# One value chain for layer one instead of two lanes of generators: two head groups in flight, outputs copied out of PSUM and gated in place

## The chip, the cores and the metric

The kernel runs on one core of a Trainium2 chip. The metric is the device time of one execution in microseconds (us), as a median over runs: 1005.12 us for the kernel before, from three runs of 1004.0, 1005.12 and 1005.37 us.

## The reference, cut to what matters

Two layers, 256 tokens, model width 2048, 16 heads of 128. The change lies in the first layer, a gated DeltaNet, between its input projection and its output projection:

```python
q, k, v = split(silu(causal_depthwise_conv(proj[..., :3 * 2048])))   # 4 taps
z = proj[..., 3 * 2048:4 * 2048]
...
o = linear attention with decay over chunks, from q, k, v            # per head
o = rms_norm(o, out_norm_w) * silu(z)
h = x + o.reshape(t, 2048) @ w_out                                   # then layer two
```

The kernel has already solved the triangular systems when the part of interest begins, and treats the 256 tokens as two blocks of 128. Per head it needs the values `v` after convolution and SiLU, a product with the inverse (twice, with a correction between them), a product with the decayed query-key matrix, a norm over 128 elements, the gate with `z`, and a transposition back to features by tokens.

## The kernel before

**The stream of weights.** 168 MB of weights pass through once, in 320 *chunks* of 512 KB, counted here from 0. `chunk` (helper `mm`, L255 in the profile) multiplies one chunk into a PSUM accumulator `psp`; there are two of those. `fetch` brings chunk i+3 when chunk i is about to be multiplied: a DMA on SP's queue into `wt` (4 buffers), a cast on ACT to a rounded copy `whi` (L206, 3 buffers), and the remainder on DVE as `wlo` (L207, 3 buffers). The cast of chunk i+3 takes the buffer that chunk i had, so it waits for the end of the matmuls that read that buffer.

**The background.** Everything else is written as generators in two lanes, `bgq` and `bg2`. After so many matmuls `tick` calls `step`, which advances one lane's first generator to its next `yield`. `yield 1` uses the step up; `yield 0` says "nothing done" and gives the step to the other lane. A scheduler then orders each engine's instructions. It may move them against the written order, matmuls of one accumulator against those of the other as well. Each engine runs its own list strictly in order.

**Chunks around the change.** Chunks 64 to 87 are z for head groups 0 to 2, 88 to 119 are v (eight chunks a group), 120 to 127 are z for group 3 (`za_small(3)`). Chunks 128 to 143 are the first half of the output projection: six chunks for accumulator 0 (128 to 133), six for accumulator 1 (134 to 139), then the last two of each (140, 141 and 142, 143). Here each chunk has 24 matmuls of 128x256 (two `whi`, one `wlo`, eight times). It reads 2 of the 16 heads of the gated output `g`, so accumulator 0 and 1 both go through head groups 0, 1, 2 (two chunks each), and chunks 140 to 143 need group 3. `ready(gmem)` writes background steps until the heads exist. `drain()` empties both lanes ahead of chunk 140.

**The value chain of one head group** (four heads, `gi` = 0 to 3):
- `v_conv` (lane `bg2`): convolution (L516, L518), one SiLU over all four heads (L806);
- `v_rest` (lane `bgq`): transposes (PE L823) and scaling (DVE L825) into `vb`; block 0 of the solve (PE L835, ACT copy L837 into `vs`); correction (PE L842, DVE L845); block 1 of the solve (L835, L837). It then puts `v_back` in lane `bg2`;
- `v_back` (lane `bg2`): output products into two PSUM tiles `po` (PE L858 to L860), squares straight from PSUM (ACT L861), their sums (DVE L868, L869), the power -0.5 on POOL (L871), scale and gate, reading `po` (DVE L885; for group 3 DVE L877), then `gated`: transposes (PE L897), and the halves of `g` (ACT L901, DVE L902).

The four work tiles `vb`, `vs`, `on`, `sq` are the same ones for each group (`dl_work(0)` to `dl_work(3)`). Two flags, `turned` and `back`, hold a group until the one ahead is far enough. For group 3 `za_small(3)`, in lane `bgq`, multiplies by z (DVE L780) and calls `gated`. All small PSUM tiles, `po` too, come from one pool `pss` of four banks.

In the profile an fp32 matmul of `order`'s lists (L835, L842, L858 to L860) shows as two instructions, a transpose as one.

Of the kernel before, what the change touches and what calls it, by code (L numbers as in the profile page):

```python
# [38 lines left out]
def tile_hybrid_trunk(  # L39
# [469 lines left out]
    def conv(src, i0):  # L509

        raw = wk("raw", 1)
        scaled(raw, src, scales["x"][1])
        cv = wk("cv")
        yield cv
        for i in range(4):
            act.activation(out=cv[:, i, :], in_=raw[:, i, :], func=AF.Copy, scale=conv_w(i0 + i, 3))  # L516
            for s in (1, 2, 3):
                dve.scalar_tensor_tensor(out=cv[:, i, s:], in0=raw[:, i, :T - s], scalar=conv_w(i0 + i, 3 - s),  # L518
                                         in1=cv[:, i, s:], op0=ALU.mult, op1=ALU.add)
# [248 lines left out]
    def za_small(gi, ps):  # L768
        if gi == 0:
            zmem["z"] = slot("kT", 16).rearrange("p (t d) -> p t d", t=2)  # L770
        for t in range(2):
            act.activation(out=zmem["z"][:, t, 512 * gi:512 * (gi + 1)], in_=ps[:, t, :], func=AF.Silu,
                           scale=scales["x"][0][:, t:t + 1])
        yield 1
        if gi == 3:
            while not gmem["on"]:
                yield 1
            on = dl_work(2)
            for t in range(2):
                dve.tensor_tensor(out=on[:, :, t, :], in0=on[:, :, t, :],  # L780
                                  in1=zmem["z"][:, t, 1536:].rearrange("p (h d) -> p h d", d=P), op=ALU.mult)
            yield 1
            yield from gated(3)
# [4 lines left out]
    def gated_tiles():  # L788
        gmem["b"] = slot("g", 32, F32R).rearrange("p (h a t) -> p h a t", h=H, a=2)
        gmem["h"], gmem["l"] = (gmem["b"][:, :, a, :] for a in range(2))  # L790
# [5 lines left out]
                step()  # L796
        return pre

    vmem = {"turned": -1, "back": -1}

    def v_conv(gi, ps):
        while vmem["turned"] < gi - 2:
            yield 1
        for cv in conv(ps, 32 + 4 * gi):
            yield 1
        act.activation(out=cv, in_=cv, func=AF.Silu)  # L806
        vmem[gi] = cv
        yield 1

    def v_rest(gi):  # L810
        while gi not in vmem:
            yield 1
        cv = vmem[gi]
        if gi == 0:
            gated_tiles()
        vb, vs, on, sq = (dl_work(k) for k in range(4))
        tt, l01, z = tmem["tt"], dl[:, :, 0, P:2 * P], zmem["z"]
        h0 = 4 * gi
        for p in range(2):
            ps = ps_small()  # L820
            for i in range(2):
                for t in range(2):
                    pe.transpose(ps[:, i * T + t * P:i * T + (t + 1) * P],  # L823
                                 cv[:, 2 * p + i, t * P:(t + 1) * P], ident)
            dve.tensor_tensor(out=vb[:, 2 * p:2 * p + 2], in0=ps.rearrange("p (h t d) -> p h t d", h=2, t=2),  # L825
                              in1=rk[:, h0 + 2 * p:h0 + 2 * p + 2, :].unsqueeze(3).broadcast_to([P, 2, 2, P]),
                              op=ALU.mult)
        vmem["turned"] = gi
        yield 1
        while vmem["back"] < gi - 1:  # L830
            yield 1
        for t in range(2):
            ps = ps_small()
            for i in range(4):
                pe.matmul(ps[:, i * P:(i + 1) * P], lhsT=tt[:, 2 * (h0 + i) + t, :], rhs=vb[:, i, t, :],  # L835
                          start=True, stop=True)
            act.copy(out=vs[:, :, t, :], in_=ps.rearrange("p (h d) -> p h d", d=P))  # L837
            yield 1
            if t == 0:
                ps = ps_small()  # L840
                for i in range(4):
                    pe.matmul(ps[:, i * P:(i + 1) * P], lhsT=l01[:, h0 + i, :], rhs=vs[:, i, 0, :],  # L842
                              start=True, stop=True)
# [4 lines left out]
                yield 1
        bg2.append(v_back(gi))

    def v_back(gi):
        vb, vs, on, sq = (dl_work(k) for k in range(4))
        z, h0 = zmem["z"], 4 * gi
        po = [ps_small(), ps_small()]
        for p in range(2):
            for i in (2 * p, 2 * p + 1):
                a, o = dec[:, h0 + i, :], po[p][:, (i % 2) * T:(i % 2 + 1) * T]
                pe.matmul(o[:, 0:P], lhsT=a[:, 0:P], rhs=vs[:, i, 0, :], start=True, stop=True)  # L858
                pe.matmul(o[:, P:T], lhsT=a[:, P:T], rhs=vs[:, i, 0, :], start=True, stop=False)
                pe.matmul(o[:, P:T], lhsT=a[:, T:T + P], rhs=vs[:, i, 1, :], start=False, stop=True)  # L860
            act.activation(out=sq[:, 2 * p:2 * p + 2], in_=po[p].rearrange("p (h t d) -> p h t d", h=2, t=2),  # L861
                           func=AF.Square)
# [6 lines left out]
        dve.scalar_tensor_tensor(out=so, in0=so, scalar=1.0 / P, in1=epq[:, h0:h0 + 4, :],  # L869
                                 op0=ALU.mult, op1=ALU.add)  # L870
        pool.tensor_tensor(out=ro, in0=so, in1=nhalf[:, :8].rearrange("p (h t) -> p h t", t=2), op=ALU.pow)  # L871
        yield 1
        yield 1
        if gi == 3:

            for p in range(2):
                dve.tensor_tensor(out=on[:, 2 * p:2 * p + 2], in0=po[p].rearrange("p (h t d) -> p h t d", h=2, t=2),  # L877
                                  in1=ro[:, 2 * p:2 * p + 2, :].unsqueeze(3).broadcast_to([P, 2, 2, P]), op=ALU.mult)
            gmem["on"] = True
            yield 1  # L880
            return
        for i in range(4):
            for t in range(2):
                c = (i % 2) * T + t * P
                dve.scalar_tensor_tensor(out=on[:, i, t, :], in0=po[i // 2][:, c:c + P], scalar=ro[:, i, t:t + 1],  # L885
                                         in1=z[:, t, (h0 + i) * P:(h0 + i + 1) * P], op0=ALU.mult, op1=ALU.mult)
        yield 1
        yield 1
        yield from gated(gi)

    def gated(gi):
        on, h0 = dl_work(2), 4 * gi
        for p in range(2):
            ps = ps_small()
            for i in range(2):
                for t in range(2):
                    pe.transpose(ps[:, i * T + t * P:i * T + (t + 1) * P], on[:, 2 * p + i, t, :], ident)  # L897
# [3 lines left out]
            act.activation(out=gh, in_=ps, func=AF.Copy, scale=sm[:, C_ONW:C_ONW + 1])  # L901
            dve.scalar_tensor_tensor(out=gl, in0=ps, scalar=sm[:, C_ONW:C_ONW + 1], in1=gh.bitcast(F32),  # L902
                                     op0=ALU.mult, op1=ALU.subtract)
        gmem["done"] = h0 + 4
        yield 1
# [350 lines left out]
```

## Time and profile before

| | |
|---|---|
| median of 3 runs | 1005.12 us |
| the profiled execution | 1003.71 us, its span 1002.0 us |
| PE matmul busy | 991.1 us, 99% |
| DVE busy | 686.0 us, 68% |
| ACT busy | 533.2 us, 53% |
| POOL busy | 71.6 us, 7% |
| mean of HBM read and written | 178 GB/s |

Busy time is what the profiler attributes to an engine. A matmul's end is modelled and overlaps the next matmul, so 99% for PE does not mean that nothing is lost; start-to-start times show more. PE's own chain makes up 95% of the chain that ended last.

### The profile page before, as it was taken

The page shows a single profiled execution, that of the slowest core. Times are in us where ns is not written, and L with a number is a line of the kernel's source. Part 1 is how long each engine was busy: PE and PEld are TensorE (multiplying, and loading weights), DVE is VectorE, ACT ScalarE, POOL GpSimd, SP SyncE. Part 2 cuts the span into 40 slices and gives each one's busy share as a digit, 9 for nine tenths or more (in the row PEclk, how much of TensorE's full clock was granted, in tenths as well). Part 3 has the DMA queues.
Part 4 walks back from the last instruction along what each step waited for, and adds up shares of the span by engine and source line. Part 5 has one row for each costly group of instructions (what it writes and reads, how often), then busy time and mean ns, then how long its engine had stood idle before and what let it go on. Part 6 is the DMA issues. An engine that isn't in the chain of part 4 may idle for free.

```text
span 1002.0 us, 15323 instructions
## 1 busy us (share of the span) xinstructions
PE 991.1 (99%) x5915; PEld 861.8 (86%) x5915; DVE 686.0 (68%) x1114; ACT 533.2 (53%) x757; POOL 71.6 (7%) x97
## 2 busy tenths in 40 slices
PE   9999999999999999999999999999999999999998
PEld 7988888888888898988888888888888888888887
DVE  7789788997999778655767555556565656555554
ACT  8456886646456555434664444446464645444442
POOL 1003000131000000001000000110101010000000
PEclk9999999999999999999999999999999999999999
DMA  9668775555765445435666766665556565555672
GB/s 290 188 174 250 208 205 153 148 169 151 205 191 169 130 145 157 141 106 169 229 188 179 233 201 212 199 177 167 175 161 187 151 188 148 168 170 172 215 218 87
DMA packets 138953, 179.67 MB, mean 179 GB/s; under 512 B 8048, under 2 KB 98560, under 8 KB 138880
## 3 DMA queue, kind: packets, MB, share of 16 engines
q1 hardware_dynamic: 136832, 172.12, 57.6%
q0 software_dynamic: 1760, 6.31, 1.8%
q8 instruction: 46, 0.75, 0.3%
q10 hardware_dynamic: 288, 0.26, 0.1%
q14 instruction: 27, 0.22, 0.1%
HBM read 176.56 MB, written 2.11 MB: 178 GB/s over the span
## 4 chain that ended last, share of the span: by engine, by line
PE 95%; ACT 1%; DVE 1%; DMA 1%; issue 1%; SPq 0%
PE psp L255 85%; PE pss L601 2%; DMA wt<-in_a_w_in_dram 1%; PE pss L255 1%; PE pss L1059 1%; PE pss L1079 1%; PE pss L1135 1%; ACT whi L206 1%; PE pss L835 1%; DVE wlo L207 1%; PE pss L1105 1%; PE pss L737 0%; PE pss L823 0%; PE pss L860 0%; PE pss L842 0%
## 5 line engine op out<-in xcount | busy, mean ns | idle before, releaser
L207 DVE TENSOR_TENSOR wlo<-wt,whi 128x1024 fp32r<-128x1024 f32 (+2 forms) x324 | 390.7, 1210 | 257.4 <-ACT whi L206 255.9
L206 ACT CAST whi<-wt 128x1024 fp32r<-128x1024 f32 (+2 forms) x324 | 336.7, 1040 | 380.5 <-PE psp L255 336.1
L255 PE MATMUL psp<-whi,xb 128*128 128x512 f32 x1024 | 319.1, 392 | 0.0
L255 PE MATMUL psp<-xb,whi 128*128 128x512 f32 (+1 forms) x1088 | 257.2, 379 | 0.5 <-ACT whi L206 0.2
L255 PEld LDWEIGHTS psp<-whi,xb 128*128 128x128 f32 x1024 | 192.1, 188 | 39.0
L255 PEld LDWEIGHTS psp<-xb,whi 128*128 128x128 f32 x1088 | 195.0, 189 | 34.7 <-ACT whi L206 0.9
L255 PE MATMUL psp<-wlo,xb 128*128 128x512 f32 x512 | 200.7, 392 | 0.0
L255 PE MATMUL psp<-xb,wlo 128*128 128x256 f32 x1024 | 147.1, 284 | 0.8 <-DVE wlo L207 0.7
L255 PEld LDWEIGHTS psp<-xb,wlo 128*128 128x128 f32 x1024 | 136.5, 191 | 7.0 <-DVE wlo L207 1.7
L255 PE MATMUL psp<-g,whi 128*128 128x512 f32 (+1 forms) x608 | 134.0, 348 | 2.2 <-ACT whi L206 1.3
L255 PEld LDWEIGHTS psp<-g,whi 128*128 128x128 f32 x608 | 104.7, 190 | 15.6 <-ACT whi L206 1.5
L255 PEld LDWEIGHTS psp<-wlo,xb 128*128 128x128 f32 x512 | 96.2, 188 | 19.4
L255 PE MATMUL psp<-g,wlo 128*128 128x256 f32 x480 | 82.5, 284 | 1.2 <-DVE wlo L207 1.2
L255 PEld LDWEIGHTS psp<-g,wlo 128*128 128x128 f32 x480 | 69.7, 191 | 3.6 <-DVE wlo L207 1.8
L518 DVE SCALAR_TENSOR_TENSOR cv<-raw,sm,cv 128x255 f32<-128x255 f32 (+2 forms) x144 | 64.3, 480 | 3.1 <-ACT cv L516 2.6
L516 ACT ACTIVATE cv<-raw,sm 128x256 f32<-128x256 f32 x48 | 22.4, 502 | 13.0 <-DVE raw L341 13.0
L326 DVE TENSOR_TENSOR ev<-psp,ev 128x512 f32<-128x512 f32 x37 | 25.2, 682 | 0.1
L325 ACT COPY ev<-psp 128x512 f32<-128x512 f32 x37 | 21.4, 579 | 2.6 <-DVE raw L341 2.5
L1042 POOL TENSOR_SCALAR ssn<-ssn,uh 128x4 f32<-128x4 f32 x16 | 9.3, 593 | 171.4 <-DVE ssn L1040 171.4
L871 POOL TENSOR_TENSOR ro<-so,nhalf 128x8 f32<-128x8 f32 x4 | 7.5, 1871 | 144.5 <-DVE so L869 144.5
L605 DVE TENSOR_TENSOR dl<-pss,dl 128x512 f32<-128x512 f32 (+1 forms) x32 | 16.4, 546 | 1.6 <-PE pss L601 1.6
L1049 DVE TENSOR_TENSOR cv<-psp,rn 128x512 f32<-128x512 f32 x16 | 10.3, 684 | 9.2 <-POOL rn L1044 9.2
(236 smaller groups left out, 730.3 us busy)
## 6 DMA issues: line engine op xcount, KB each, us to landing
wt<-in_b_w_in_dram SPq DMA_DIRECT2D x128, 512.0 KB, 3.8
wt<-in_a_w_in_dram SPq DMA_DIRECT2D x125, 512.0 KB, 4.0
wt<-in_a_w_out_dram SPq DMA_DIRECT2D x32, 512.0 KB, 3.6
wt<-in_b_w_out_dram SPq DMA_DIRECT2D x32, 512.0 KB, 3.5
tt<-line POOLq DMA_DIRECT2D x4, 512.0 KB, 8.4
dl<-in_xT_dram POOLq DMA_DIRECT2D x4, 512.0 KB, 6.3
dl<-in_relb_dram POOLq DMA_DIRECT2D x4, 512.0 KB, 4.9
g<-in_xT_dram SPq DMA_DIRECT2D x7, 256.0 KB, 6.4
```

The lines of the kernel that those rows point to most:

```text
L206: cast = act.copy(out=hi[:, js, cs], in_=wt[:, js, cs])
L207: rest = dve.tensor_tensor(out=lo[:, js, cs], in0=wt[:, js, cs], in1=hi[:, js, cs].bitcast(F32), op=ALU.subtract)
L255: state["mm"] = pe.matmul(*args, **kw).ins
L325: act.copy(out=ev, in_=ps[:, :, 1, :])
L326: dve.tensor_tensor(out=ev, in0=ps[:, :, 0, :], in1=ev, op=ALU.add)
L516: act.activation(out=cv[:, i, :], in_=raw[:, i, :], func=AF.Copy, scale=conv_w(i0 + i, 3))
L518: dve.scalar_tensor_tensor(out=cv[:, i, s:], in0=raw[:, i, :T - s], scalar=conv_w(i0 + i, 3 - s), in1=cv[:, i, s:], op0=ALU.mult, op1=ALU.add)
L601: pe.matmul(dst, lhsT=kq[:, a, i, c:c + P], rhs=rhs, start=(n == 0), stop=(n == 2))
L605: dve.tensor_tensor(out=dl[:, h, :, c], in0=src.rearrange("p (k c) -> p k c", k=2), in1=dec[:, h, c].unsqueeze(1).broadcast_to([P, 2, n]), ...
L835: pe.matmul(ps[:, i * P:(i + 1) * P], lhsT=tt[:, 2 * (h0 + i) + t, :], rhs=vb[:, i, t, :], start=True, stop=True)
L1049: dve.tensor_tensor(out=n[:, t, :].rearrange("p (h d) -> p h d", d=P), in0=ps[:, t, :].rearrange("p (h d) -> p h d", d=P), in1=rn[:, t, :] ...
L1059: pe.transpose(pt[:, i * T + t * P:i * T + (t + 1) * P], n[:, t, c:c + P], ident)
```

## The change

`v_rest` and `v_back` become one generator `v_chain` in lane `bgq`, written for all groups: transposes of group gi, outputs of group gi-1, solve of group gi, gate of group gi-1. Two groups are in flight, so `vb` alternates between two work tiles, and `vs` of groups 1 to 3 lies in `tt`, over the inverse blocks that the group before has used up. The flag `back` goes; waiting generators give their step away (`yield 0`). The SiLU is issued in two halves, as soon as two heads are convolved. The outputs are copied from PSUM into `on` (ACT L862), squared from there (L863), and scaled and gated in place in `on`. `za_small(3)` moves to lane `bg2`.

```diff
     def za_small(gi, ps):
...
             while not gmem["on"]:
-                yield 1
+                yield 0
...
     def v_conv(gi, ps):
         while vmem["turned"] < gi - 2:
-            yield 1
-        for cv in conv(ps, 32 + 4 * gi):
-            yield 1
-        act.activation(out=cv, in_=cv, func=AF.Silu)
+            yield 0
+        for n, cv in enumerate(conv(ps, 32 + 4 * gi)):
+            if n in (2, 4):
+                act.activation(out=cv[:, n - 2:n], in_=cv[:, n - 2:n], func=AF.Silu)
+            yield 1
         vmem[gi] = cv
...
+    def v_bufs(gi):
+
+        vb = dl_work(3 * (gi % 2))
+        vs = dl_work(1) if gi == 0 else tmem["tt"][:, 8 * gi - 8:8 * gi, :].rearrange("p (h t) d -> p h t d", t=2)
+        return vb, vs, dl_work(2)
...
-        while vmem["back"] < gi - 1:
-            yield 1
...
-        bg2.append(v_back(gi))
-
-    def v_back(gi):
-        vb, vs, on, sq = (dl_work(k) for k in range(4))
-        z, h0 = zmem["z"], 4 * gi
-        po = [ps_small(), ps_small()]
+
+    def v_out(gi):
+        (sq, vs, on), h0 = v_bufs(gi), 4 * gi
         for p in range(2):
+            po, pair2 = ps_small(), slice(2 * p, 2 * p + 2)
             for i in (2 * p, 2 * p + 1):
-                a, o = dec[:, h0 + i, :], po[p][:, (i % 2) * T:(i % 2 + 1) * T]
+                a, o = dec[:, h0 + i, :], po[:, (i % 2) * T:(i % 2 + 1) * T]
...
-            act.activation(out=sq[:, 2 * p:2 * p + 2], in_=po[p].rearrange("p (h t d) -> p h t d", h=2, t=2),
-                           func=AF.Square)
-        vmem["back"] = gi
-        yield 1
-
+            act.copy(out=on[:, pair2], in_=po.rearrange("p (h t d) -> p h t d", h=2, t=2))
+            act.activation(out=sq[:, pair2], in_=on[:, pair2], func=AF.Square)
+            yield 1
+
+    def v_gate(gi):
+        (sq, _, on), h0, z = v_bufs(gi), 4 * gi, zmem["z"]
...
-                dve.scalar_tensor_tensor(out=on[:, i, t, :], in0=po[i // 2][:, c:c + P], scalar=ro[:, i, t:t + 1],
+                dve.scalar_tensor_tensor(out=on[:, i, t, :], in0=on[:, i, t, :], scalar=ro[:, i, t:t + 1],
                                          in1=z[:, t, (h0 + i) * P:(h0 + i + 1) * P], op0=ALU.mult, op1=ALU.mult)
...
+    def v_chain():
+        for gi in range(5):
+            if gi < 4:
+                yield from v_turn(gi)
+            if gi == 0:
+                gated_tiles()
+            if gi:
+                yield from v_out(gi - 1)
+            if gi < 4:
+                yield from v_solve(gi)
+            if gi:
+                yield from v_gate(gi - 1)
...
         bg2.append(v_conv(gi, ps))
-        bgq.append(v_rest(gi))
-    bgq.append(za_small(3, block("tokens", xb, 2)))
+        if gi == 0:
+            bgq.append(v_chain())
+    bg2.append(za_small(3, block("tokens", xb, 2)))
```

The lines of the chain move a little: L823, L835, L842, L858 to L860, L897 of before are L824, L838, L845, L859 to L861, L910 after on PE; L837, L861, L901 become L840, L862 with L863, and L914 on ACT; L825, L845, L868, L885, L877, L902 become L826, L848, L870, L886, L879, L915 on DVE.

**Where instructions stand.** First place: PE in the output projection, after the fourth chunk of accumulator 0. Buffer numbers are kept here: `psp_4433` and `psp_4434` are accumulators 0 and 1 before, `psp_4445` and `psp_4446` after; the number of `whi` tells the chunk. Before (`whi_4436` is chunk 131, `whi_4544` chunk 134):

```order
L255 MATMUL psp_4433<-g_3455,whi_4436 128x256 x2
L255 MATMUL psp_4433<-g_3455,wlo_4437 128x256
L835 MATMUL pss_4063<-dl_109,tt_2498 128x128
L858 MATMUL pss_4073<-dl_109 128x128
L859 MATMUL pss_4073<-dl_109 128x128
L858 MATMUL pss_4074<-dl_109 128x128
L859 MATMUL pss_4074<-dl_109 128x128
L835 MATMUL pss_4063<-dl_109,tt_2498 128x128 x3
L255 MATMUL psp_4434<-g_3455,whi_4544 128x256 x2
L255 MATMUL psp_4434<-g_3455,wlo_4545 128x256
```

After (`whi_4448` is chunk 131, `whi_4496` and `whi_4526` are 132 and 133, `whi_4556` is 134):

```order
L861 MATMUL pss_4366<-tt_2498,dl_109 128x128
L255 MATMUL psp_4445<-g_3446,whi_4428 128x256 x2
L255 MATMUL psp_4445<-g_3446,wlo_4429 128x256
L255 MATMUL psp_4445<-g_3446,whi_4448 128x256 x2
...
L255 MATMUL psp_4445<-g_3446,whi_4496 128x256 x2
...
L255 MATMUL psp_4445<-g_3446,whi_4526 128x256 x2
...
L255 MATMUL psp_4446<-g_3446,whi_4556 128x256 x2
```

Before, PE leaves accumulator 0 after chunk 131 and goes to chunks 134, 135 and 136 of accumulator 1, while 132 and 133, already cast, wait for head group 2. After, chunks 131, 132, 133 and 134 follow each other.

Second place: PE at the last transposes of the chain, those of head group 3. Before (`whi_4694` is chunk 139, `whi_4724` chunk 140):

```order
L255 MATMUL psp_4434<-g_3455,wlo_4695 128x256
L897 MATMUL pss_4463<-ident_94,dl_109 128x128
L897 MATMUL pss_4470<-ident_94,dl_109 128x128
L897 MATMUL pss_4463<-ident_94,dl_109 128x128 x3
L897 MATMUL pss_4470<-ident_94,dl_109 128x128 x3
L255 MATMUL psp_4433<-g_3455,whi_4724 128x256
```

After (`whi_4586` is chunk 135, `whi_4616` chunk 136, `whi_4736` chunk 140):

```order
L255 MATMUL psp_4446<-g_3446,whi_4586 128x256 x2
L910 MATMUL pss_4475<-ident_94,dl_109 128x128
L910 MATMUL pss_4482<-ident_94,dl_109 128x128
...
L910 MATMUL pss_4475<-ident_94,dl_109 128x128 x3
L910 MATMUL pss_4482<-ident_94,dl_109 128x128 x3
...
L255 MATMUL psp_4446<-g_3446,whi_4616 128x256 x2
...
L255 MATMUL psp_4445<-g_3446,whi_4736 128x256 x2
```

Before, the transposes stand directly ahead of the first chunk that needs them; after, they stand inside chunk 135, with 105 matmuls between them and chunk 140.

Third place: ACT between the casts of chunks 116 and 118 or 119, where group 0 is solved and put out. Before:

```order
L206 CAST whi<-wt 128x1024 x2
L837 COPY dl<-pss 128x4x128
L806 ACTIVATE cv<-cv 128x1024
L206 CAST whi<-wt 128x1024
L325 COPY ev<-psp 128x512
L861 ACTIVATE dl<-pss 128x2x2x128 x2
L206 CAST whi<-wt 128x1024 x3
```

After:

```order
L206 CAST whi<-wt 128x1024 x2
L840 COPY dl<-pss 128x4x128
L806 ACTIVATE cv<-cv 128x512
L862 COPY dl<-pss 128x2x2x128
L863 ACTIVATE dl<-dl 128x2x2x128
L862 COPY dl<-pss 128x2x2x128
L863 ACTIVATE dl<-dl 128x2x2x128
L840 COPY tt<-pss 128x4x128
L206 CAST whi<-wt 128x1024
```

Before, the cast of chunk 118 stands ahead of the two squares; after, it stands behind seven small instructions, six of which wait for PE, directly or through the one ahead.

More of the change, by code (lines that the diff above doesn't have):

```diff
@@ L797, in ready, with v_turn @@
         return pre
-    vmem = {"turned": -1, "back": -1}
+    vmem = {"turned": -1}
     def v_conv(gi, ps):
         while vmem["turned"] < gi - 2:
+            yield 0
+        for n, cv in enumerate(conv(ps, 32 + 4 * gi)):
+            if n in (2, 4):
+                act.activation(out=cv[:, n - 2:n], in_=cv[:, n - 2:n], func=AF.Silu)
             yield 1
-        for cv in conv(ps, 32 + 4 * gi):
-            yield 1
-        act.activation(out=cv, in_=cv, func=AF.Silu)
         vmem[gi] = cv
-        yield 1
-    def v_rest(gi):
-        while gi not in vmem:
-            yield 1
-        cv = vmem[gi]
-        if gi == 0:
-            gated_tiles()
-        vb, vs, on, sq = (dl_work(k) for k in range(4))
-        tt, l01, z = tmem["tt"], dl[:, :, 0, P:2 * P], zmem["z"]
-        h0 = 4 * gi
+    def v_bufs(gi):
+        vb = dl_work(3 * (gi % 2))
+        vs = dl_work(1) if gi == 0 else tmem["tt"][:, 8 * gi - 8:8 * gi, :].rearrange("p (h t) d -> p h t d", t=2)
+        return vb, vs, dl_work(2)
+    def v_turn(gi):
+        while gi not in vmem:
+            yield 0
+        cv, (vb, _, _), h0 = vmem[gi], v_bufs(gi), 4 * gi
         for p in range(2):
@@ L829, in v_rest, with v_solve @@
         yield 1
-        while vmem["back"] < gi - 1:
-            yield 1
+    def v_solve(gi):
+        (vb, vs, _), h0 = v_bufs(gi), 4 * gi
+        tt, l01 = tmem["tt"], dl[:, :, 0, P:2 * P]
         for t in range(2):
@@ L848, in v_rest @@
                 yield 1
-        bg2.append(v_back(gi))
-    def v_back(gi):
-        vb, vs, on, sq = (dl_work(k) for k in range(4))
-        z, h0 = zmem["z"], 4 * gi
-        po = [ps_small(), ps_small()]
+    def v_out(gi):
+        (sq, vs, on), h0 = v_bufs(gi), 4 * gi
         for p in range(2):
+            po, pair2 = ps_small(), slice(2 * p, 2 * p + 2)
             for i in (2 * p, 2 * p + 1):
-                a, o = dec[:, h0 + i, :], po[p][:, (i % 2) * T:(i % 2 + 1) * T]
+                a, o = dec[:, h0 + i, :], po[:, (i % 2) * T:(i % 2 + 1) * T]
                 pe.matmul(o[:, 0:P], lhsT=a[:, 0:P], rhs=vs[:, i, 0, :], start=True, stop=True)
@@ L860, in v_back @@
                 pe.matmul(o[:, P:T], lhsT=a[:, T:T + P], rhs=vs[:, i, 1, :], start=False, stop=True)
-            act.activation(out=sq[:, 2 * p:2 * p + 2], in_=po[p].rearrange("p (h t d) -> p h t d", h=2, t=2),
-                           func=AF.Square)
-        vmem["back"] = gi
-        yield 1
+            act.copy(out=on[:, pair2], in_=po.rearrange("p (h t d) -> p h t d", h=2, t=2))
[3 more added lines that the diff above has]
+        (sq, _, on), h0, z = v_bufs(gi), 4 * gi, zmem["z"]
         so = tiny.tile([P, 4, 2], F32, name="so", tag="so")
@@ L872, in v_back @@
         yield 1
-        yield 1
         if gi == 3:
             for p in range(2):
-                dve.tensor_tensor(out=on[:, 2 * p:2 * p + 2], in0=po[p].rearrange("p (h t d) -> p h t d", h=2, t=2),
-                                  in1=ro[:, 2 * p:2 * p + 2, :].unsqueeze(3).broadcast_to([P, 2, 2, P]), op=ALU.mult)
+                pair2 = slice(2 * p, 2 * p + 2)
+                dve.tensor_tensor(out=on[:, pair2], in0=on[:, pair2],
+                                  in1=ro[:, pair2, :].unsqueeze(3).broadcast_to([P, 2, 2, P]), op=ALU.mult)
             gmem["on"] = True
@@ L883, in v_back @@
             for t in range(2):
-                c = (i % 2) * T + t * P
-                dve.scalar_tensor_tensor(out=on[:, i, t, :], in0=po[i // 2][:, c:c + P], scalar=ro[:, i, t:t + 1],
+                dve.scalar_tensor_tensor(out=on[:, i, t, :], in0=on[:, i, t, :], scalar=ro[:, i, t:t + 1],
                                          in1=z[:, t, (h0 + i) * P:(h0 + i + 1) * P], op0=ALU.mult, op1=ALU.mult)
         yield 1
-        yield 1
         yield from gated(gi)
+    def v_chain():
[10 more added lines that the diff above has]
+                yield from v_gate(gi - 1)
     def gated(gi):
```

## The prediction

> **What bounds the kernel now.** I read the page's engine rows first, then what PE waits for, then PE's stretches, then PE's instructions in time.
>
> ```profile
> PE   991.1 (99%) x5915; PEld 861.8 (86%) x5915; DVE 686.0 (68%) x1114; ACT 533.2 (53%) x757; POOL 71.6 (7%) x97
> PE psp L255 <- DVE wlo L207: 1.9, 5, 1.0
> PE psp L255 <- ACT whi L206: 1.5, 2, 1.3
> PE pss L897 <- DVE dl L780: 1.5, 2, 1.3
> 370.00:395.00 25.00, 25.00 (x150) 22.14 (x149) 22.62 (x42) 13.99 (x19) 2.57 (x1) 1.00 0.47 139
> 430.00:440.00 10.00, 7.76 (x64) 7.16 (x63) 5.21 (x12) 3.76 (x5) 1.64 (x1) 1.00 0.26 87
> 460.00:470.00 10.00, 7.77 (x60) 6.90 (x59) 6.59 (x10) 3.36 (x4) 3.31 (x3) 1.00 0.45 139
> 420.00:470.00 50.00, 45.28 (x371) 43.44 (x370) 25.88 (x41) 17.63 (x22) 4.95 (x4) 1.00 0.38 120
> ```
>
> In the rows of the windows the first two figures are the window and its length; then come PE, PEld, DVE, ACT and POOL busy with their counts, PE's granted clock, DMA share and GB/s. PE is the bound nearly everywhere at a clock of 1.00, and the change alters none of its matmuls. It can pay only where PE stands still, and that is in the stretch it touches: PE is idle 4.7 us of 420 to 470, most of it in two windows, while 370 to 395, where the chain also runs, has no idle time. The waits there are for a cast, a remainder and the last gate.
>
> What the stretch loses in all I take from start times, since the modelled ends hide part of each gap. The counts from the first matmul of chunk 128 (410.52) to the first of chunk 144 (478.46):
>
> ```profile
> 410.52 0.40 PE L255 MATMUL psp<-g,whi 128*128 128x256 f32 x2
> 478.46 0.63 PE L255 MATMUL psp<-g,whi 128*128 128x512 f32 x2
> L255 PE MATMUL psp<-g,whi 128*128 128x256 f32 x256 | 49.0, 288 | 2.0 <-ACT whi L206 1.3 <-ACT g L901 0.5 <-DVE g L902 0.3
> L255 PE MATMUL psp<-g,wlo 128*128 128x256 f32 x128 | 36.7, 287 | 1.2 <-DVE wlo L207 1.2
> L835 PE MATMUL pss<-dl,tt 128*128 128x128 f32 x32 | 4.9, 274 | 0.0
> L897 PE MATMUL pss<-ident,dl 128*128 128x128 f32 x24 | 4.8, 279 | 1.5 <-DVE dl L780 1.5
> L859 PE MATMUL pss<-dl 128*128 128x128 f32 x16 | 3.1, 275 | 0.0
> L823 PE MATMUL pss<-ident,cv 128*128 128x128 f32 x16 | 2.6, 272 | 0.0
> L842 PE MATMUL pss<-dl 128*128 128x128 f32 x16 | 2.1, 275 | 0.0
> 445.42 3.11 PE psp L255 x26
> 448.53 0.89 PE pss L842 x8
> ```
>
> The last two rows, from the chain in order of time, give the pace: 3.11 / 26 = 0.120 us for a 128x256 matmul, 0.89 / 8 = 0.111 for a small one. So 384 x 0.120 + 136 x 0.111 (32 + 24 + 16 + 16 + 16 and twice 16 of L858 and L860, as many as L859) = 46.1 + 15.1 = 61.2 us of work in 67.9 us: **6.7 us are lost**. Where:
>
> ```profile
> 427.24 0.48 PE L255 MATMUL psp<-g,whi 128*128 128x256 f32 x2
> 427.97 0.39 PE L255 MATMUL psp<-g,wlo 128*128 128x256 f32 x1 [0.25 <-DVE wlo L207]
> 432.38 0.28 PE L255 MATMUL psp<-g,wlo 128*128 128x256 f32 x1
> 432.83 1.04 ACT L206 CAST whi<-wt 128x1024 fp32r<-128x1024 f32 x1
> 434.11 1.22 DVE L207 TENSOR_TENSOR wlo<-wt,whi 128x1024 fp32r<-128x1024 f32 x1
> 435.38 0.39 PE L255 MATMUL psp<-g,wlo 128*128 128x256 f32 x1 [0.95 <-DVE wlo L207]
> 462.78 0.28 PE L255 MATMUL psp<-g,wlo 128*128 128x256 f32 x1
> 463.64 1.29 DVE L780 TENSOR_TENSOR dl<-dl,kT 128x512 f32<-128x512 f32 x2
> 467.10 0.39 PE L255 MATMUL psp<-g,whi 128*128 128x256 f32 x1 [0.29 <-DVE g L902]
> ```
>
> - 427.24 to 427.97: two matmuls need 0.24, so 0.5 is lost; 432.38 to 435.38: three need 0.36, so 2.6 is lost. This is the jump to accumulator 1. Chunks 132 and 133 hold two of three `whi` and `wlo` buffers until head group 2 exists, so chunks 134 and 135 share the third: the cast at 432.83 starts when chunk 134 lets go, PE gets its `wlo` only 2.55 us later.
> - 462.78 to 467.10: one matmul, eight transposes, two matmuls are 0.12 + 0.89 + 0.24 = 1.25; so **3.1** is lost. Group 3's gate ends last and PE has nothing else.
> - The remaining 0.5 lies about the transposes of group 2 and small switches.
>
> **The change part by part.** The profiled execution took 1003.71 us for a span of 1002.0, 1.4 under the median of the runs (1005.12); I sum against 1003.71 and add 1.4.
>
> Durations that the sum uses (rows of 345 to 470):
>
> ```profile
> L207 DVE TENSOR_TENSOR wlo<-wt,whi 128x1024 fp32r<-128x1024 f32 x31 | 37.8, 1223 | 29.1 <-ACT whi L206 29.1
> L206 ACT CAST whi<-wt 128x1024 fp32r<-128x1024 f32 x31 | 32.5, 1049 | 42.9 <-PE psp L255 40.9 <-ACT cv L516 2.0
> L837 ACT COPY dl<-pss 128x512 f32<-128x512 f32 x8 | 4.7, 587 | 9.0 <-PE pss L835 9.0
> L861 ACT ACTIVATE dl<-pss 128x512 f32<-128x512 f32 x8 | 4.8, 598 | 6.5 <-PE pss L860 6.5
> L516 ACT ACTIVATE cv<-raw,sm 128x256 f32<-128x256 f32 x8 | 3.9, 506 | 4.3 <-DVE raw L341 4.3
> L806 ACT ACTIVATE cv<-cv 128x1024 f32<-128x1024 f32 x2 | 2.1, 1058 | 0.7 <-DVE cv L518 0.7
> L901 ACT ACTIVATE g<-pss,sm 128x512 fp32r<-128x512 f32 x8 | 5.2, 684 | 2.7 <-PE pss L897 2.7
> L871 POOL TENSOR_TENSOR ro<-so,nhalf 128x8 f32<-128x8 f32 x4 | 7.5, 1871 | 144.5 <-DVE so L869 144.5
> L885 DVE SCALAR_TENSOR_TENSOR dl<-pss,ro,kT 128x128 f32<-128x128 f32 x24 | 6.5, 343 | 3.3 <-POOL ro L871 3.3
> ```
>
> 1. *Two groups in flight, `yield 0`, lane of z3*: the order after runs chunks 131 to 134 in sequence. Group 2's transposes now stand in chunk 130, a whole chunk and the outputs of group 3 ahead of chunk 132; what follows them is 2 x 0.68 on ACT and two like it on DVE, under 3 us, against about 7 us of PE work. Three buffers rotate again: **-3.1** (0.5 + 2.6).
> 2. *The end of the chain*: 105 matmuls, 12.6 us, cover the same 3 us after group 3's transposes, which are not waited for by chunk 140: **-3.1**. What is late next is nothing that I find: the residual's first step needs accumulator 0, as before.
> 3. *Eight copies out of PSUM* on ACT: 8 x 0.59 = 4.7. A square from SBUF lies between L516 (0.51 for half the width) and L806 (1.06 for double), 0.69 by a line through both: 8 x 0.09 = +0.7. SiLU halves by the same line: 8 x 0.69 for 4 x 1.06, +1.3. ACT gets 6.7 us more. From 420 on it is busy 17.6 of 50, from 370 to 395 14.0 of 25; a cast (1.05) and a remainder (1.22) have two chunks (5.7 us) and the small matmuls between. Cost 0, if the queue's order keeps it hidden; uncovered all 6.7.
> 4. *Gate from SBUF*: 24 operations of 0.27 (L885's busy 6.5 / 24), the same width and count from SBUF. Bounds: up to 0.1 more or less each, 2.4 us of DVE in all over 100 us in which it has a third free; I take 0, since none of it lies on PE's path. The two of group 3 likewise.
> 5. *Small tiles*: `po` no longer holds two of four banks from output to gate, over POOL's 1.9 us; the copy frees one about 1 us after its last matmul. Worth 0 by itself, since PE showed no wait for a bank.
> 6. *What waits behind the new instructions.* ACT now has seven instructions ahead of the cast of chunk 118. I walked the order from the start of chunk 115 (PE's paces, the durations above): PE ends the outputs 7.0 us in; ACT ends the second square at about 8.5, the copy behind it at 9.1, the cast at 10.2; DVE ends the remainder at 11.4. Chunk 118 starts at 14.6: **3.2 us to spare**. On the same walk DVE, which also has the convolution of group 3 between chunks 120 and 124, delivers chunk 124's remainder with 1.3 us to spare, and frees the banks for group 1's outputs 1.7 early. Nobody is late, so 0, but this is the thin place. POOL and SP keep their order.
>
> Sum: -3.1 - 3.1 and 0 for the rest = **-6.2**: 997.5, or **998.9** as a median. The lower bound is all 6.7 us, 998.4, less the 1.1 by which the lowest run of before lies under its median: 997.3; I take 0.5 more for a chip's spread, 996.8.
>
> **The rivals.**
>
> *Part is given back at the thin places.* DVE is at 22.6 of 25 us from 370 to 395 and gets work of groups 2 and 3 earlier. A wait on DVE of 2.5 us more than walked (an activation late for a convolution step, a power late for a gate) makes chunk 124 and group 1's outputs about 1 us late each, and the same again a group later: 2 to 4 us back, 1001 to 1003. For it: the share; against: the same stretch before held 90% with no idle PE.
>
> *The copies land on the path*, so the change doesn't do what it says. Only two operations read an output after the copy, and the 6.7 us of point 3 can end ahead of a wait of PE each time: -6.2 + 6.7 = +0.5, a median of 1005.6, or, with half of it, 1002.3. For: ACT's queue is in order and PE's `whi` passes through it. Against: ACT waited 40.9 us for PE ahead of 31 casts. The Trainium skill says the same in general ("VectorE: DVE Perf Modes", section "Rules for kernel authors"): on matmul output, accept the slower PSUM source, or copy to SBUF first if many operations follow. Here one square and one gate follow, so by that rule the copy costs; the idle ACT in the rows speaks for its being hidden, and 1005.6 is what the rule would give.
>
> *Slower than before*: the bank behind the outputs. Group 1's outputs (chunk 120) need banks that DVE frees with its two L902 steps, which stand among convolution steps that wait for ACT, and ACT's casts stand behind the copies that wait for those outputs. If DVE comes more than 1.7 us late, PE stops and the lateness comes round to the next cast. From 4.5 us late on, in each of groups 1 to 3, PE loses 3 x 2.8 = 8.4 us: 998.9 + 8.4 = 1007.3. For: the loop exists in the order. Against: before, with four banks and `po` held longer, PE never waited for one.
>
> **How the numbers follow.** A measurement of this kernel tells about 0.2%, 2.0 us, from no change: faster is below 1003.1, slower above 1007.1. All of the gain (997 to 1000): 0.65. Part given back (1000 to 1003): 0.20. Copies on the path (1002 to 1006): 0.10, mostly no measurable change. Bank loop: 0.05. Faster is 0.65, 0.20 and little of the third, 0.85; same 0.10; slower 0.05. The range from 996.8 to 1002.0 holds the first case and most of the second; the first alone is 996.8 to 1000.
>
> **What would show it.** Right: from chunk 128 to 144 PE needs about 61.5 us for what order leaves there, no wait of L255 for `wlo` or `whi` over 0.5 us between 420 and 470, the last transposes without a wait for L780, and the residual's first row about 6 us earlier. Wrong in step 6: PE idle between 370 and 415, behind L207 or L915. Wrong in 1: PE waiting for `g` at chunk 132. The prediction falls if casts begin late behind L862 and L863 and PE's idle time moves forward instead of going.

## The result: 997.5 us, and the profile after

| | before | after |
|---|---|---|
| median of 6 runs each | 1005.02 us (1003.81 to 1005.37) | 997.5 us (997.03 to 998.12) |
| the profiled execution, its span | 1003.71, 1002.0 us | 998.12, 996.4 us |
| ratio | | 0.9928, 95% interval 0.9916 to 0.9941 |

The change saves 7.5 us between the medians, 5.9 to 8.4 us by the interval; 6.2 were forecast. One execution below, of the kernel with one SiLU over four heads, ran at a granted clock of 0.557 and took 1647.57 us; it is left out of that kernel's median.

The page of the changed kernel, its row of engines; then the same four stretches as before (window, length, busy time of PE, PEld, DVE, ACT and POOL with counts, PE's granted clock, DMA share, GB/s):

```profile
PE 990.2 (99%) x5915; PEld 862.7 (87%) x5915; DVE 685.7 (69%) x1114; ACT 537.3 (54%) x769; POOL 71.2 (7%) x97
```

```profile
370.00:395.00 25.00, 25.00 (x172) 22.87 (x171) 18.48 (x35) 14.41 (x24) 2.57 (x1) 1.00 0.37 108
430.00:440.00 10.00, 10.00 (x88) 10.00 (x87) 5.06 (x6) 5.25 (x8) 0.00 (x0) 1.00 0.42 136
460.00:470.00 10.00, 10.00 (x86) 10.00 (x85) 6.00 (x7) 4.53 (x7) 0.75 (x1) 1.00 0.63 196
420.00:470.00 50.00, 50.00 (x421) 49.88 (x420) 30.21 (x41) 23.52 (x30) 6.42 (x5) 1.00 0.56 181
```

PE is busy for all of 420 to 470, with 421 matmuls where it had 371. DVE and ACT have more to do in that stretch than before (30.2 and 23.5 us for 25.9 and 17.6), and none of it is waited for. PE's waits of the whole execution are these, and not one lies between 345 and 500 us:

```profile
PE pss L89 <- DVE kT L82: 1.3, 1, 1.3
PE psp L255 <- DVE wlo L207: 0.6, 3, 0.2
PE psp L255 <- DVE ev L326: 0.4, 2, 0.2
PE psp L255 <- ACT whi L206: 0.3, 1, 0.3
```

The time line at five places: the first matmul of chunk 128, group 3's product with z (L780) and last `g` (L915), chunk 140, the first step of the residual (L969, which was L955), chunk 144.

```profile
420.60 0.40 PE L255 MATMUL psp<-g,whi 128*128 128x256 f32 x2
443.94 1.29 DVE L780 TENSOR_TENSOR dl<-dl,kT 128x512 f32<-128x512 f32 x2
449.34 1.41 DVE L915 SCALAR_TENSOR_TENSOR g<-pss,sm,g 128x512 fp32r<-128x512 f32 x2 [0.88 <-ACT g L914]
461.34 0.40 PE L255 MATMUL psp<-g,whi 128*128 128x256 f32 x2
467.30 0.15 DVE L969 COPY dl<-psp 1x1 f32<-1x1 f32 x1 [0.69 <-PE psp L255]
472.86 0.63 PE L255 MATMUL psp<-g,whi 128*128 128x512 f32 x2
```

The last `g` is there at 450.75; chunk 140 starts at 461.34, 10.6 us later. Before, L780 ran at 463.64 and chunk 140 waited for it. From chunk 128 to chunk 144 PE takes 472.86 - 420.60 = 52.3 us for 384 matmuls of 128x256 and 56 small ones: 384 x 0.120 + 56 x 0.111 = 52.3. Nothing is lost there, where 6.7 us were. The other 80 small matmuls now stand ahead of chunk 128.

How the pair of profiled executions adds up: just ahead of chunk 112 the changed kernel's was later by 1.02 us (before first, then after).

```profile
354.62 0.62 PE L255 MATMUL psp<-xb,whi 128*128 128x512 f32 x2
```

```profile
355.64 0.62 PE L255 MATMUL psp<-xb,whi 128*128 128x512 f32 x2
```

At chunk 144 it is earlier by 478.46 - 472.86 = 5.6 us, which is also what the spans differ by. So the region gave **6.6 us**, the 6.7 that PE had lost in it. The 1.02 us arose ahead of the region; runs of the unchanged kernel, below, start that chunk up to 1.15 us later than its first profile too.

### The profile page after: what moved, and what is told of

It reads as the page before. It is cut to its first block, busy times and chain, and to the rows that moved or that the text cites. A ratio compares the mean times of both kernels' runs of the same rounds, so it can differ in the third digit from the quotient of the medians.

```text
span 996.4 us, 15340 instructions
## 1 busy us (share of the span) xinstructions
PE 990.2 (99%) x5915; PEld 862.7 (87%) x5915; DVE 685.7 (69%) x1114; ACT 537.3 (54%) x769; POOL 71.2 (7%) x97
## 4 chain that ended last, share of the span: by engine, by line
PE 97%; ACT 1%; DMA 1%; issue 1%; DVE 0%; SPq 0%
PE psp L255 86%; PE pss L601 2%; PE pss L255 1%; PE pss L838 1%; PE pss L1073 1%; PE pss L1093 1%; PE pss L1149 1%; DMA g<-in_xT_dram 1%; PE pss L1119 1%; ACT whi L206 1%; PE pss L737 0%; PE pss L824 0%; PE pss L845 0%; PE pss L861 0%; PE pss L860 0%
## 5 line engine op out<-in xcount | busy, mean ns | idle before, releaser
L207 DVE TENSOR_TENSOR wlo<-wt,whi 128x1024 fp32r<-128x1024 f32 (+2 forms) x324 | 390.9, 1210 | 248.2 <-ACT whi L206 246.7
L255 PE MATMUL psp<-whi,xb 128*128 128x512 f32 x1024 | 320.3, 392 | 0.0
L255 PE MATMUL psp<-xb,whi 128*128 128x512 f32 (+1 forms) x1088 | 258.3, 381 | 0.5 <-ACT whi L206 0.3
L255 PEld LDWEIGHTS psp<-xb,whi 128*128 128x128 f32 x1088 | 196.0, 190 | 34.7 <-ACT whi L206 0.8
L255 PEld LDWEIGHTS psp<-whi,xb 128*128 128x128 f32 x1024 | 192.1, 188 | 38.8
L255 PE MATMUL psp<-wlo,xb 128*128 128x512 f32 x512 | 200.9, 392 | 0.0
L255 PE MATMUL psp<-xb,wlo 128*128 128x256 f32 x1024 | 147.5, 285 | 0.7 <-DVE wlo L207 0.6
L255 PEld LDWEIGHTS psp<-xb,wlo 128*128 128x128 f32 x1024 | 137.0, 191 | 7.0 <-DVE wlo L207 1.8
L255 PE MATMUL psp<-g,whi 128*128 128x512 f32 (+1 forms) x608 | 131.6, 347 | 0.2 <-DVE ev L326 0.2
L255 PEld LDWEIGHTS psp<-g,whi 128*128 128x128 f32 x608 | 104.4, 190 | 13.0 <-DVE ev L326 0.6
L255 PEld LDWEIGHTS psp<-wlo,xb 128*128 128x128 f32 x512 | 96.2, 188 | 19.3
L255 PE MATMUL psp<-g,wlo 128*128 128x256 f32 x480 | 82.3, 283 | 0.0
L255 PEld LDWEIGHTS psp<-g,wlo 128*128 128x128 f32 x480 | 69.8, 191 | 1.8
```

The source lines that it names most:

```text
L207: rest = dve.tensor_tensor(out=lo[:, js, cs], in0=wt[:, js, cs], in1=hi[:, js, cs].bitcast(F32), op=ALU.subtract)
L255: state["mm"] = pe.matmul(*args, **kw).ins
```

## The experiments

All kernels here compute the reference in full. Those with a ratio were timed beside 15 or 17 runs of the kernel before on their chip (medians 1004.02 and 1004.01 us).

**The changed kernel with one group after the other** (the copies, the lane of z and the SiLU halves stay):

```diff
-        for gi in range(5):
-            if gi < 4:
-                yield from v_turn(gi)
+        for gi in range(4):
+            yield from v_turn(gi)
...
-            if gi:
-                yield from v_out(gi - 1)
-            if gi < 4:
-                yield from v_solve(gi)
-            if gi:
-                yield from v_gate(gi - 1)
+            yield from v_solve(gi)
+            yield from v_out(gi)
+            yield from v_gate(gi)
```

> The kernel after, but v_chain runs one head group after the other (turn, solve, outputs, gate of group 0, then of group 1 and so on); the copies out of PSUM, the split SiLU, yield 0 and the lane of z3 stay. Theory A (the gain is PE's two standstills in the output projection, and they go because two groups are in flight): the order again leaves accumulator 0 after chunk 131 and puts the last transposes directly ahead of chunk 140, so PE waits for a cast and a remainder near chunk 134 (2 to 3 us) and for the last gate (3 us or more): 1003 to 1006 us, no gain. Theory B (the copies free PSUM banks and that makes the chain fast enough): about 998.

Measured: 1014.63 us, ratio 1.0095 (1.0079 to 1.0111), some 17 us over the changed kernel and 10 over the kernel before. Both standstills return, as A says, but the size was missed. PE's waits from 345 to 500, and three stretches:

```profile
PE pss L906 <- DVE dl L780: 6.2, 1, 6.2
PE psp L255 <- DVE wlo L207: 1.3, 3, 0.8
PE psp L255 <- ACT whi L206: 1.0, 1, 1.0
PE pss L838 <- DVE dl L826: 0.8, 1, 0.8
```

```profile
460.00:470.00 10.00, 6.28 (x54) 6.08 (x53) 3.75 (x4) 4.56 (x7) 1.27 (x1) 1.00 0.34 112
470.00:480.00 10.00, 7.39 (x31) 6.39 (x32) 4.00 (x6) 1.33 (x2) 2.03 (x3) 0.55 0.45 136
480.00:490.00 10.00, 10.00 (x78) 9.91 (x78) 7.16 (x12) 6.40 (x12) 0.76 (x1) 0.93 0.55 166
```

The wait for the last gate is 6.2 us (1.5 before), and a second cost comes behind it: the granted clock falls to 0.55 in 470 to 480, and PE gets through 31 matmuls in the 7.4 us in which it is busy there.

**The kernel before with the copies alone:**

```diff
-            act.activation(out=sq[:, 2 * p:2 * p + 2], in_=po[p].rearrange("p (h t d) -> p h t d", h=2, t=2),
-                           func=AF.Square)
+            act.copy(out=on[:, 2 * p:2 * p + 2], in_=po[p].rearrange("p (h t d) -> p h t d", h=2, t=2))
+            act.activation(out=sq[:, 2 * p:2 * p + 2], in_=on[:, 2 * p:2 * p + 2], func=AF.Square)
...
-                dve.scalar_tensor_tensor(out=on[:, i, t, :], in0=po[i // 2][:, c:c + P], scalar=ro[:, i, t:t + 1],
+                dve.scalar_tensor_tensor(out=on[:, i, t, :], in0=on[:, i, t, :], scalar=ro[:, i, t:t + 1],
```

(L877 likewise.)

> The kernel before with one edit: its outputs are copied out of PSUM at once, squared and gated from the copy; lanes, steps and SiLU as before. Theory A (the copies neither pay nor cost in place; the order of the groups pays): PE keeps its jump past chunks 132 and 133 and the wait for the last gate, which may grow by the copy's 0.59 us ahead of the square; 1004 to 1007 us. Rival B (the early release of the banks brings the chain forward): about 998 us.

Measured: 1013.5 us, ratio 1.0084 (1.007 to 1.0098). Both expectations missed: the copies alone cost 9.5 us between the medians (7.0 to 9.8 by the interval). The end of the chain in time, and the clock, in that kernel:

```profile
464.94 0.57 ACT L861 COPY dl<-pss 128x512 f32<-128x512 f32 x1
465.54 0.63 ACT L862 ACTIVATE dl<-dl 128x512 f32<-128x512 f32 x1
466.21 1.22 DVE L868 TENSOR_REDUCE so<-dl 128x8 f32<-128x1024 f32 x1 [2.08 <-ACT dl L862]
467.56 1.23 DVE L207 TENSOR_TENSOR wlo<-wt,whi 128x1024 fp32r<-128x1024 f32 x1
468.70 0.16 DVE L869 SCALAR_TENSOR_TENSOR so<-so,epq 128x8 f32<-128x8 f32 x1
469.00 1.64 POOL L871 TENSOR_TENSOR ro<-so,nhalf 128x8 f32<-128x8 f32 x1 [29.74 <-DVE so L869]
470.67 1.29 DVE L877 TENSOR_TENSOR dl<-dl,ro 128x512 f32<-128x512 f32 x2 [1.81 <-POOL ro L871]
472.00 1.29 DVE L780 TENSOR_TENSOR dl<-dl,kT 128x512 f32<-128x512 f32 x2
472.75 1.50 PE L897 MATMUL pss<-ident,dl 128*128 128x128 f32 x5 [6.19 <-DVE dl L780]
```

```profile
436.00:440.00 4.00, 2.38 (x18) 1.97 (x16) 2.51 (x3) 1.07 (x2) 1.64 (x1) 1.00 0.39 130
440.00:444.00 4.00, 3.84 (x22) 3.84 (x22) 2.21 (x9) 0.00 (x0) 0.00 (x0) 0.62 0.43 131
472.00:478.00 6.00, 5.11 (x20) 4.12 (x21) 2.70 (x4) 1.33 (x2) 1.67 (x2) 0.50 0.16 19
```

Each copy puts 0.57 us ahead of its square and so of the group's sums (L868); for group 3 the sums' last step (L869) then falls behind a remainder (L207). With one group at a time the next group's transposes come after the gate of the one ahead, so lateness is handed on. It does not grow by a fixed amount per group: the sums of groups 0 to 3 start 2.3, 3.7, 3.1 and 7.3 us later than in the profile of before, and the largest step, from group 2 to 3, has the first stretch of low clock in it. L780 ends up at 472.00 (463.64 before).

At chunk 144 this execution is 9.9 us late (488.38 for 478.46). PE's waits from 345 to 500 account for 4.5 of them: they come to 9.3 us, where the profile of before has 4.8. The two stretches at a low clock account for some 4.0, an estimate from the rows above, busy time by what the clock lacks of 1.00 (3.84 x 0.38 + 5.11 x 0.50). So about half of the price of the copies is waiting, and most of the rest is the clock behind it. The chain one group at a time with copies costs about the same in either code: 1013.5 and 1014.6.

**The changed kernel without the copies** (the outputs stay in PSUM, as before; two groups in flight):

```diff
...
-            act.copy(out=on[:, pair2], in_=po.rearrange("p (h t d) -> p h t d", h=2, t=2))
-            act.activation(out=sq[:, pair2], in_=on[:, pair2], func=AF.Square)
+            act.activation(out=sq[:, pair2], in_=po.rearrange("p (h t d) -> p h t d", h=2, t=2), func=AF.Square)
...
-                dve.scalar_tensor_tensor(out=on[:, i, t, :], in0=on[:, i, t, :], scalar=ro[:, i, t:t + 1],
+                c = (i % 2) * T + t * P
+                dve.scalar_tensor_tensor(out=on[:, i, t, :], in0=vmem["po", gi, i // 2][:, c:c + P], scalar=ro[:, i, t:t + 1],
```

> The kernel after, but the outputs stay in PSUM until the gate reads them, as before (no copy, the square reads PSUM): 8 ACT copies of 0.58 us less, two of the four small banks held longer. Theory A: chunks 128 to 143 keep their sequence, the last transposes stand in chunk 134, no standstill: 997 to 999 us, like the kernel after. Theory B: the banks are missing, PE waits for them in chunks 120 to 130, and 2 to 6 us come back: 1000 to 1004.

**The changed kernel with each copy made twice** (one more line `act.copy` in `v_out`):

> The kernel after with each copy out of PSUM issued twice: 8 more ACT copies of 0.58 us, 4.7 us of ACT. If the copies are hidden beside PE: 997 to 998.5 us. If they lie on the path, as the prediction's second rival has it: about 1002.

Measured: 997.38 us, ratio 0.9933 (0.992 to 0.9945), without copies, and 997.39 us, 0.9931 (0.9918 to 0.9945), with twice as many. With doubled copies PE has no idle time from 345 to 470 either, though ACT does 67.2 us of work there. The rows for that stretch, of the changed kernel and then of the one with doubled copies:

```profile
345.00:470.00 125.00, 125.00 (x903) 116.93 (x902) 84.45 (x136) 62.75 (x88) 10.84 (x7) 1.00 0.50 152
```

```profile
345.00:470.00 125.00, 125.00 (x903) 116.91 (x903) 84.75 (x138) 67.24 (x97) 8.97 (x7) 1.00 0.50 151
```

So with two groups in flight the copies are neither needed nor felt; the same eight instructions cost 9.5 us, the clock's part included, where the groups come one by one.

**The kernel before, with chunks 132 and 133 in memory of their own**, so that they no longer hold two of three buffers:

```diff
-        hi = wst.tile([P, kc, width], F32R, name="whi", tag="whi")
-        lo = wst.tile([P, kc, width], F32R, name="wlo", tag="wlo")
+        if i in (132, 133):
+            if i == 132:
+                state["xs"] = slot("xb", 32, F32R).rearrange("p (n k w) -> p n k w", n=8, k=kc)
+            hi, lo = (state["xs"][:, 2 * (i - 132) + n] for n in range(2))
+        else:
+            hi = wst.tile([P, kc, width], F32R, name="whi", tag="whi")
+            lo = wst.tile([P, kc, width], F32R, name="wlo", tag="wlo")
```

> The kernel before, but whi and wlo of chunks 132 and 133 lie in memory of their own (the tile of the layer's inputs, free by then), so that they hold no buffer of the rotation while they wait for head group 2. Theory A: the jump to accumulator 1 stays in the order and its wait for a cast and a remainder (2.6 + 0.5 us) goes; the wait for the last gate (3.1 us) stays: 1002 us, if the chain moves up with PE. If the chain's own length sets its end, the last wait grows by what the first one gave: 1005. Rival (the jump itself, not the buffers, costs the time): 1005 with the wait near chunk 134 still there.

Measured: 1006.12 us, ratio 1.0016 (1.0008 to 1.0025): no gain. PE's waits from 345 to 500 and two stretches:

```profile
PE pss L902 <- DVE dl L785: 4.4, 2, 4.2
PE pss L847 <- ACT dl L842: 0.2, 1, 0.2
```

```profile
430.00:440.00 10.00, 10.00 (x87) 10.00 (x87) 6.49 (x14) 4.04 (x6) 1.64 (x1) 1.00 0.37 118
460.00:470.00 10.00, 5.49 (x23) 4.54 (x23) 5.13 (x7) 2.33 (x3) 3.06 (x3) 0.75 0.34 95
```

The first standstill is gone: 430 to 440 is full, and no wait for `wlo` is left. But the chain's end has not moved, and PE only comes to it sooner:

```profile
463.49 1.29 DVE L785 TENSOR_TENSOR dl<-dl,kT 128x512 f32<-128x512 f32 x2
464.24 0.44 PE L902 MATMUL pss<-ident,dl 128*128 128x128 f32 x2 [4.20 <-DVE dl L785]
467.88 0.63 PE L260 MATMUL psp<-g,whi 128*128 128x256 f32 x2
468.31 0.41 PE L260 MATMUL psp<-g,wlo 128*128 128x256 f32 x1
```

L785 (L780 of before) starts at 463.49 instead of 463.64, so the 3 us saved in front are waited off here. Behind that a pair of matmuls takes 0.63 instead of 0.40: the clock again, at 0.75 over 460 to 470. All 11 runs of this kernel list a mean granted clock of 0.995 to 0.998.

**The kernel before with `yield 0` alone** (the four `yield 1` of waiting generators in the value path):

> The kernel before with one edit: waiting generators of the value path yield 0 instead of 1, so a wait no longer uses up a step; groups still run one after the other in two lanes. Theory A (the gain comes from group 3's chain starting while group 2's is under way): PE's order still jumps from chunk 131 to 134 and the last transposes stand directly ahead of chunk 140, so both standstills stay and the time is that of before within 0.2%, 1002 to 1006 us. Rival B (steps wasted by waiting were what delayed the chain): faster by most of the gain, about 998 us.

Measured: 1004.86 us, ratio 0.9999 (0.9989 to 1.0008): A. Giving steps away does nothing by itself.

**The changed kernel with z of group 3 back in the chain's lane** (`bgq.append(za_small(3, ...))`), **and with one SiLU over four heads** (`if n == 4: act.activation(out=cv, in_=cv, func=AF.Silu)`):

> The changed kernel with za_small(3) back in the lane of the chain. Theory A (two groups in flight are enough): the order still takes chunks 131 to 134 in sequence and the last transposes stand ahead of chunk 137; 997 to 998.5 us, as the changed kernel. Rival B (the move of z for group 3 to the other lane is what brings the last gate forward): the 3.1 us ahead of chunk 140 return, 1000 to 1002 us.

> The changed kernel with one SiLU over all four heads, as before. Theory A: as the changed kernel, 997 to 998.5 us, since the start of a group's transposes is not what ends last. Rival B (the halves let the transposes of a group begin two convolution steps earlier, and the chain's end needs that): part of the last wait returns, 999 to 1001 us.

Measured: 996.71 us, 0.9922 (0.9908 to 0.9935), and 997.23 us (five executions), 0.9925 (0.9911 to 0.994). Neither differs from the changed kernel's 0.9928 (0.9916 to 0.9941) by what can be told. The comparison of the second rests on times alone. Both side edits are free, each taken out by itself; the two groups in flight without any of the side edits were not run. No version is shown to be faster than the change.

**The kernel before, three times more.** Its runs spread from 1003.3 to 1006.4 us, those of the changed kernel only from 997.0 to 998.1. That asked for a cause:

> The kernel before, unchanged, profiled again. Theory A (its runs fall into two groups, about 1003.7 and 1005.3 us, because a standstill of PE near 433 or 463 us is in some executions followed by a stretch at half the granted clock): a profiled execution under 1004.5 us has a granted clock of 1.00 in 430 to 440 and 460 to 480, one above it has a lower clock in one of these windows, and its later chunks are later by half that stretch. Rival B (the spread comes from the DMA waits of the first 20 us): the clock is 1.00 in both kinds and the difference stands already at 345 us.

> As for the run ahead: the kernel before, unchanged. A: under 1004.5 us no stretch at half clock between 420 and 480, above it one; B: the difference stands already at 345 us and the clock is 1.00.

> As for the two runs ahead: the kernel before, unchanged. A: under 1004.5 us no stretch at half clock between 420 and 480, above it one; B: the difference stands already at 345 us and the clock is 1.00.

Measured: 1004.9, 1005.7 and 1003.74 us. In that order, PE ahead of chunk 112 and in 434 to 442:

```profile
355.77 0.62 PE L255 MATMUL psp<-xb,whi 128*128 128x512 f32 x2
434.00:442.00 8.00, 5.95 (x45) 5.39 (x46) 6.06 (x13) 3.35 (x5) 1.64 (x1) 1.00 0.21 67
```

```profile
355.18 0.62 PE L255 MATMUL psp<-xb,whi 128*128 128x512 f32 x2
434.00:442.00 8.00, 6.57 (x40) 6.30 (x41) 4.89 (x12) 2.06 (x3) 1.64 (x1) 0.79 0.22 67
```

```profile
354.64 0.62 PE L255 MATMUL psp<-xb,whi 128*128 128x512 f32 x2
```

Both theories hold, each for one run. The first is 1.15 us late already ahead of chunk 112 (354.62 in the profile of before) at a clock of 1.00: B, as far as the place and the clock go; that the DMA waits of the first 20 us cause it is not shown. The second is 0.56 late there; then its clock is 0.79 in 434 to 442, and at chunk 144 it is 1.97 late (480.43 for 478.46), so that stretch cost it 1.4 us: A. The third is as the profile of before throughout. The `yield 0` kernel, on time ahead of chunk 112 (354.63), shows the same fall to 0.79 in 434 to 442 and is 1.21 us late at chunk 144 (479.67).

Every run beside the experiments lists the mean granted clock of its whole execution, and that tells how often it falls:

| kernel before, 32 runs | runs | us | median |
|---|---|---|---|
| mean clock 0.999 or 1.000 | 19 | 1003.26 to 1004.62 | 1003.71 |
| mean clock 0.998 or lower | 13 | 1004.76 to 1008.16 | 1005.53 |

The two groups of A are there, they do not overlap, and they differ by 1.8 us. The runs of the changed kernel and of its four versions with two groups in flight, 27 without the one left out above, all list 0.999 or 1.000. The first run above (1004.9 us at 1.00) shows that a run can also be late without the clock.

## Why the prediction was right, step by step

*What bounds the kernel* held: the gain came from PE's standstills, all 6.7 us of them, and from nowhere else inside the region.

*Step 1, -3.1*: chunks 131 to 134 follow one another without a wait, and nothing is lost at the jump. Held in the sum, but the term does not stand alone, as I had it. With only the buffers freed, the gain was given back at the last gate and the kernel was 0.16% slower. It counts because step 2 makes room behind it; step 2 by itself was not run.

*Step 2, -3.1*: held with much to spare. I gave it 12.6 us of matmuls as cover after the transposes; from the last `g` to chunk 140 10.6 us stay free. The change moves the last gate's product with z from 463.64 to 443.94, by 20 us, of which about 7 can be used.

*Step 3, copies and squares at 0*: held, and the doubled copies show how safe it was. The sizes: a copy 0.58 (0.59 taken), a square from SBUF 0.63 (0.69 taken), half a SiLU 0.62 (0.69 taken).

```profile
L863 ACT ACTIVATE dl<-dl 128x512 f32<-128x512 f32 x8 | 5.1, 631 | 0.2
L862 ACT COPY dl<-pss 128x512 f32<-128x512 f32 x8 | 4.7, 582 | 11.5 <-PE pss L861 11.2
L806 ACT ACTIVATE cv<-cv 128x512 f32<-128x512 f32 x4 | 2.5, 624 | 0.0
L886 DVE SCALAR_TENSOR_TENSOR dl<-dl,ro,kT 128x128 f32<-128x128 f32 x24 | 6.6, 344 | 1.5 <-POOL ro L873 1.5
```

By these rows the copies, the squares and the SiLU halves add 4.7 + 0.3 (5.1 for 4.8) + 0.8 (8 x 0.62 for 4 x 1.06) = 5.8 us, where 6.7 were forecast; ACT's busy time on the page grew by 4.1 (533.2 to 537.3). What I had not seen is that this 0 depends on steps 1 and 2; without them the copies cost 9.5.

*Step 4, gate from SBUF at 0*: 344 ns for 343. *Step 5, banks at 0*: no wait for one, and without the copies, with banks held as long as before, the time is the same.

*Step 6, the thin places*: the walk was close at chunk 118 and too tight at 124. The cast of chunk 118 starts at 373.95 and its remainder ends at 376.26, 3.5 us ahead of the chunk (3.2 walked); chunk 124's remainder ends at 400.20, 3.2 us ahead (1.3 walked).

```profile
373.95 1.05 ACT L206 CAST whi<-wt 128x1024 fp32r<-128x1024 f32 x1
375.03 1.23 DVE L207 TENSOR_TENSOR wlo<-wt,whi 128x1024 fp32r<-128x1024 f32 x1
398.99 1.21 DVE L207 TENSOR_TENSOR wlo<-wt,whi 128x1024 fp32r<-128x1024 f32 x1
```

*The signs*: no wait of L255 between 420 and 470, the last transposes without a wait for L780, and the residual's first row at 467.30 for 473.02, 5.7 us earlier. "About 61.5 us from chunk 128 to 144" was wrong as a number: the order leaves 56 small matmuls there, not 136, so 52.3 it was; I had not counted them.

*The rivals*: no time was given back at thin places, and no bank loop showed. That the copies land on the path fell for this kernel. The Trainium skill's rule ("VectorE: DVE Perf Modes", section "Rules for kernel authors": take the slower PSUM source unless many operations follow) is borne out where the chain is serial, by 9.5 us, and makes no difference where it is not (997.38 against 997.5). That PSUM is the slower source is not seen in the gate, 343 ns from PSUM and 344 from SBUF.

*The size*: 6.2 forecast, 6.6 in the region, 7.5 between the medians. The 0.4 is the small rest that I left out of the sum. The other 0.9 is for the most part the clock. In two of five profiled executions with the old standstill (the three above, the profile of before and the `yield 0` kernel) it fell behind the standstill, for 1.2 to 1.4 us, and the changed kernel has no standstill for it to follow. Over the 32 runs of the table, the mean (1004.57) lies 0.8 above that of the 19 whose clock did not fall (1003.76). Of the six runs of before in the result the clock is not on record; four of them took 1004.99 to 1005.37, as runs with a lower clock do.

This also shows which term of the forecast was mis-sized. I summed against 1003.71, an execution at a clock of 1.00, and then added 1.4 to come to a median, without a cause for the 1.4. The changed kernel did not keep them: 1003.71 - 6.2 is 997.5, and 998.9 was forecast. That this agrees to the tenth is luck, since single executions differ by up to 1.15 us already ahead of the region.

## What to carry to other kernels

Ask of each wait whether it ends a chain of its own or only passes time until the next wait: of two waits in front of the same serial chain, the first was worth nothing by itself here, since freeing it merely lengthened the second. Where a chain of small steps crosses engines once per group, try to start the next group before the last has ended; here copies, halves and lanes then made no measurable difference, while in the serial form two copies of 0.57 us per group came back as 9.5, about half of it waiting and most of the rest the clock. Judge an instruction's price in the order that it will run in, not by its duration.

## What the hardware showed beyond that

A standstill of PE can cost more than its length. After a wait of 6.2 us (copies alone in the old order) the granted clock was 0.50 in 472 to 478. After one of 4.2 us (chunks 132 and 133 in their own memory) it was 0.50 from 466 to 470, and pairs of 128x256 matmuls took 0.43 us from start to start instead of 0.24, until 471.72. From 466.50 on that is 5.2 us of matmuls at about 0.213 each where 0.120 is the pace; an estimate of the loss is (1 - 0.120 / 0.213) x 5.2 = 2.3 us. The Trainium skill says so in general ("TensorE: Matmul & The Clock Gate", section "What's actually happening": half the clock after an idle window of about 3.4 us, counted in a free-running window), and these two agree. The old standstill, told below, is shorter than that, and the clock fell behind it too in some executions. All 11 runs of the kernel with the wait of 4.2 us list a mean clock of 0.995 to 0.998, and all 11 of the two kernels with the wait of 6.2 us one of 0.993 to 0.996.

The old standstill, stretches of 1.4 and 1.2 us about two matmuls at 432 to 435 us, is well under the 4.2 us. Still it was followed by a lower clock in two of the five profiled executions that have it, and 13 of the 32 runs of the kernel before list a lower mean clock; the 3.1 us lost at 463, with eight transposes in them, were followed by none in the five. So a gap of 1.4 us was not safe with another of 1.2 close behind it, and whether the clock falls differs from one execution to the next. What decides it is not shown.
